# Regrouping the columns of an attention projection into panels of 512, 328, 512, 512 and 256, and loading the first tokens in two halves

## The chip, the cores and the metric

The kernel is written for Trainium2 and runs on one core. The metric is the device time of one execution, in microseconds (us). All times below come from timed runs of this kernel or from one execution that was taken with the hardware profiler.

## What is computed

The program is a decoder trunk of two layers over 512 tokens of width 1024, in float32. The change lies in the first layer's token mixer, a sparse attention:

```python
proj = x @ w_in                                   # 512 x 1024 times 1024 x 2120
q, k, v, iq, ik, iw = jnp.split(proj, A_SPLITS, axis=-1)   # 1024, 256, 256, 512, 64, 8 columns
q, k, iq, ik = partial_rotary(...)                # first 16 of the 64 numbers of each head
# for each block of 128 queries:
s = einsum('bqhd,bsd->bqhs', iq_b, ik) * IDX_DIM ** -0.5
score = einsum('bqh,bqhs->bqs', iw_b, relu(s))    # 8 index heads
_, sel = lax.top_k(where(causal, score, -inf), 128)
p = softmax(q_b @ k_sel)                          # 16 heads, 4 key heads
out = (p @ v_sel) @ w_o
x = layer_norm(alpha * x + out)
```

The 128 best keys of a query are all its causal keys for the first block of 128 queries. So token tile 0 needs no index queries and no index weights; it needs its index key, because later blocks look at it.

## The kernel before

**Tiles.** The 512 tokens are four token tiles of 128. `XT` holds x transposed, in a high and a low float32r part. A weight panel is up to 512 columns of a weight matrix over all 1024 rows. It comes as four units of 256 rows: `fetch` (L116) loads a unit into one of four `raw` buffers with one DMA on the queue of SyncE for each range of columns, and `split` (L125) makes the high part on ScalarE (L130) and the low part on VectorE (L131), into one of six `w` buffers. `natural` (L198) multiplies one token tile with a panel: 8 slices of 128 rows times three products (L186 to L188), so 24 matmuls whose length is the panel's width, into one of three PSUM tiles `ps`. `to_xt` (L223) turns a token tile into `XT` with 8 transposes, two ScalarE copies (L233) and two VectorE subtractions (L234). `next_panel` loads one panel ahead.

**Panels of the projection.** Five panels: 264 columns (three index query heads, the index key, the index weights), 320 columns (five index query heads), 512 (keys and values), 512 (query heads 0 to 7), 512 (query heads 8 to 15). Token tiles go in the order 1, 2, 3, 0 through the first panel (L632). Tile 0 takes only 64 of its columns there (L638), and the second panel leaves tile 0 out (L648). The panel list stands at L1074.

**After a product.** `rotated` (L546) copies and rotates the heads: one ScalarE copy (L554), three VectorE operations (L557 to L559). `stack_q` and `stack_k` split the result in two parts (L566 and L567; L584 to L586) and put transposes off by `depth` products (`later`, L190), which go to `iqT`, `ikT`, `kT` or `qT` through ScalarE (L575, L596).

**Selection and attention.** `index_scores(b)` (L616) makes the scores of block b, 8 heads with two matmuls, a ScalarE Relu and a VectorE accumulation each. It needs `iqT` of tile b and `ikT` of tiles 0 to b, so the first call stands behind the panels that hold the index queries and the index keys. `top_k` (L663) then takes 16 rounds of a maximum and a replacement on VectorE for each of the blocks 1 to 3 (L668, L669), closed by L671. `blocks` (L778) is a generator of 16 items, one for each block and key head: logits (L691 to L699), transposes of the weights (L706), the product with the values, and, at the end of a block, `to_xt` of its output. Items 8 to 11 are block 2 and items 12 to 15 block 3. Block 2 needs the selection of block 2, block 3 that of block 3. The code asks for all selections before item 8.

**Order.** SyncE's DMAs go in the order in which the program issues them. For the compute engines the framework takes the program and lays out each engine's order ahead of the run: earlier code comes first where it is ready by its own estimate, and later code moves forward where it isn't. The first product of the third panel, for example, stands on TensorE ahead of the first index scores, which the code names before it. Around the attention's end the code is:

```python
wu = self.next_panel()
for _ in range(A_KV):
    item()                      # items 8 to 11
self.load_residual(x)
for t in range(NT - 1):
    item()                      # items 12 to 14
    self.out_first(wu, t)       # output projection, first half, tile t
for _ in bl:
    pass
self.out_first(wu, NT - 1)
```

Of the kernel before, what the change touches and what calls it, by code (L numbers as in the profile page):

```python
# [23 lines left out]
P = 128  # L24
# [70 lines left out]
class Trunk:  # L95
# [29 lines left out]
    def split(self, src):  # L125
# [4 lines left out]
        self.nc.scalar.copy(hi, src)  # L130
        self.nc.vector.tensor_sub(lo, src, hi.bitcast(F32))  # L131
        return hi, lo

    def _load(self, i):
# [4 lines left out]
        for ci, (w, r0, nk, cols) in enumerate(panel):  # L139
            for u in range(nk // 2):  # L140
                hi, lo = self.split(self.fetch(w, r0 + 2 * u * P, cols))
                for j in range(2):
                    units[(ci, 2 * u + j)] = (hi[:, j, :], lo[:, j, :])
# [21 lines left out]
    def prefetch(self, n):  # L165
        while len(self.loaded) < min(len(self.panels), n):
            self.loaded.append(self._load(len(self.loaded)))
# [378 lines left out]
    def rotated(self, src, t, h):  # L546
# [3 lines left out]
        dst = self.rt.tile([P, self.rt_h, 64], F32, name="nat")[:, :h, :]  # L550
# [4 lines left out]
        a = self.rt.tile([P, self.rt_h, 2, 8], F32, name="rot_c")  # L555
        b = self.rt.tile([P, self.rt_h, 2, 8], F32, name="rot_s")
# [5 lines left out]
    def stack_q(self, nat, h, dst):  # L562

        nc = self.nc
        hl = self.rt.tile([P, self.rt_h, P], F32R, name="hl")
# [13 lines left out]
    def stack_k(self, nat, h, dst):  # L579

        nc = self.nc
        hl = self.rt.tile([P, h, 2, 2, 64], F32R, name="dup")
# [17 lines left out]
    def attention(self, x, xs):  # L600

        nc, tc = self.nc, self.tc
        with tc.tile_pool(name="att", bufs=1) as ap:
# [5 lines left out]
            with tc.tile_pool(name="idx", bufs=1) as ip, tc.tile_pool(name="ir", bufs=2) as it, \  # L609
                    tc.tile_pool(name="idt", bufs=3) as self.rt:  # L610
# [3 lines left out]
                self.rt_h, self.depth = 5, 2  # L614
# [17 lines left out]
                for i, t in enumerate(ORDER):  # L632
                    def turn_next(i=i):
                        if i + 1 < NT:
                            self.to_xt(xs[ORDER[i + 1]], ORDER[i + 1])
                    ik = ikT[:, None, :, t * P:(t + 1) * P]
                    if t == 0:
                        ps = self.natural(u, t, 192, 64)  # L638
                        self.stack_k(self.rotated(ps[:, 0:64], t, 1), 1, ik)
                    else:  # L640
                        ps = self.natural(u, t, 0, 264, turn_next)
                        nat = self.rotated(ps[:, 0:256], t, 4)
                        self.stack_q(nat[:, 0:3, :], 3, iqT[:, t - 1, 5:8, :])
                        self.stack_k(nat[:, 3:4, :], 1, ik)
                        nc.vector.tensor_scalar(iw[:, t, :], ps[:, 256:264], IDX_H ** -0.5, A_D ** -0.5,
# [524 lines left out]
```

## Time and profile before

| what | value |
|---|---|
| median of 3 runs | 1160.45 us (1160.43 to 1160.72) |
| profiled execution, own time | 1162.37 us |
| span of its profile | 1160.6 us |
| TensorE matmul busy | 1144.4 us, 99% |
| TensorE weight loads busy | 963.0 us, 83% |
| VectorE busy | 890.5 us, 77% |
| ScalarE busy | 556.9 us, 48% |
| granted TensorE clock, mean | 0.996 |

A share is that of the whole span, and matmuls overlap in the pipeline, so that a busy TensorE can still hide short waits. Where TensorE really runs without a break is seen from the distance between the starts of successive matmuls. PEclk is the granted share of TensorE's full clock of 2.4 GHz; 0.50 is 1.2 GHz.

### The profile page before, as it was taken

Reading aid. Unit: us, or ns where it says so; the run is one execution under the profiler, and the core shown is the slowest. Engines: PE = TensorE matmul, PEld = TensorE weight load, DVE = VectorE, ACT = ScalarE, POOL = GpSimd, SP = SyncE. Lnnn points to the kernel's source line nnn. Section 1 sums busy time; section 2 is a strip of 40 time slices with the busy share of each in tenths; the row PEclk is TensorE's granted clock in tenths of the full one; section 3 lists DMA queues with packets and bytes.
Section 4 is the critical chain, followed back from the end, with each engine's and each line's share of the span. In section 5 each row is a group of like instructions: output and inputs, shape, how many; then the busy total and the mean of one; then the engine's idle time right before and its main releaser. Section 6 shows DMA issues by size and latency. Waiting matters only on the chain. (4 is left out here: it accounts for less than half of the span.)

```text
span 1160.6 us, 15685 instructions
## 1 busy us (share of the span) xinstructions
PE 1144.4 (99%) x5847; PEld 963.0 (83%) x5847; DVE 890.5 (77%) x1587; ACT 556.9 (48%) x953; POOL 212.3 (18%) x144
## 2 busy tenths in 40 slices
PE   8999999999999999999999999999999999999997
PEld 7877888888888888888888998888988888888875
DVE  6799997687886786687864577766697866886787
ACT  6665786544444353344355444343453534444342
POOL 0000000002213203212302254110032032213221
PEclk9999999999999999999999999999999999999998
DMA  7322130521431441242241231233223422431421
GB/s 245 100 73 73 37 110 1 160 87 37 145 106 42 143 140 62 90 145 86 74 133 50 64 112 35 70 109 110 74 60 122 145 70 76 145 107 46 138 73 73
DMA packets 58196, 109.35 MB, mean 94 GB/s; under 512 B 5204, under 2 KB 10712, under 8 KB 58120
## 3 DMA queue, kind: packets, MB, share of 16 engines
q1 hardware_dynamic: 56968, 104.16, 28.1%
q0 software_dynamic: 1152, 4.19, 1.3%
q8 instruction: 46, 0.75, 0.3%
q14 instruction: 30, 0.25, 0.1%
HBM read 106.24 MB, written 2.10 MB: 93 GB/s over the span
## 5 line engine op out<-in xcount | busy, mean ns | idle before, releaser
L131 DVE TENSOR_TENSOR w_lo<-raw,w_hi 128x1024 fp32r<-128x1024 f32 (+4 forms) x220 | 289.3, 1333 | 27.5 <-ACT w_hi L130 25.1
L130 ACT CAST w_hi<-raw 128x1024 fp32r<-128x1024 f32 (+4 forms) x220 | 223.4, 1024 | 121.4 <-PE ps L188 43.8
L186 PE MATMUL ps<-XT,w_hi 128*128 128x512 f32 (+1 forms) x640 | 236.1, 369 | 0.0
L187 PE MATMUL ps<-XT,w_hi 128*128 128x512 f32 (+1 forms) x640 | 235.7, 368 | 0.0
L188 PE MATMUL ps<-XT,w_lo 128*128 128x512 f32 (+1 forms) x640 | 235.6, 368 | 0.0
L186 PE MATMUL ps<-w_hi,XT 128*128 128x512 f32 (+5 forms) x440 | 164.5, 374 | 0.8 <-ACT w_hi L130 0.8
L187 PE MATMUL ps<-w_lo,XT 128*128 128x512 f32 (+5 forms) x440 | 161.8, 368 | 1.1 <-DVE w_lo L131 1.1
L188 PE MATMUL ps<-w_hi,XT 128*128 128x512 f32 (+5 forms) x440 | 161.6, 368 | 0.0
L186 PEld LDWEIGHTS ps<-XT,w_hi 128*128 128x128 f32 x640 | 120.7, 189 | 20.2 <-issue 0.2
L187 PEld LDWEIGHTS ps<-XT,w_hi 128*128 128x128 f32 x640 | 120.7, 189 | 20.2 <-issue 0.4
L188 PEld LDWEIGHTS ps<-XT,w_lo 128*128 128x128 f32 x640 | 120.7, 189 | 20.1 <-issue 0.2
L152 POOL TENSOR_TENSOR raw<-raw 128x1024 f32<-128x1024 f32 x14 | 34.2, 2440 | 385.4 <-DVE w_lo L131 385.4
L186 PE MATMUL ps<-w_hi,form 128*128 128x512 f32 x260 | 102.3, 393 | 0.7 <-DVE big L408 0.7
L187 PE MATMUL ps<-w_lo,form 128*128 128x512 f32 x260 | 101.5, 390 | 0.0
L188 PE MATMUL ps<-w_hi,form 128*128 128x512 f32 x260 | 101.4, 390 | 0.0
L187 PEld LDWEIGHTS ps<-w_lo,XT 128*128 128x128 f32 x440 | 83.5, 190 | 11.9 <-DVE w_lo L131 1.7
L186 PEld LDWEIGHTS ps<-w_hi,XT 128*128 128x128 f32 x440 | 83.5, 190 | 11.5 <-ACT w_hi L130 1.0
L188 PEld LDWEIGHTS ps<-w_hi,XT 128*128 128x128 f32 x440 | 83.5, 190 | 10.8
L131 DVE TENSOR_TENSOR w_lo<-t,w_hi 128x1024 fp32r<-128x1024 f32 x14 | 30.4, 2168 | 72.7 <-ACT w_hi L130 72.7
L360 DVE TENSOR_TENSOR h<-h 128x512 f32<-128x512 f32 (+1 forms) x72 | 43.7, 624 | 44.1 <-ACT h L359 44.1
L359 ACT ACTIVATE h<-ps 128x512 f32<-128x512 f32 (+1 forms) x72 | 38.7, 546 | 61.7 <-PE ps L188 54.7
L130 ACT CAST w_hi<-t 128x1024 fp32r<-128x1024 f32 x14 | 14.7, 1051 | 105.2 <-POOL t L154 105.2
(238 smaller groups left out, 1986.1 us busy)
## 6 DMA issues: line engine op xcount, KB each, us to landing
raw<-in_mlp_w_up_dram SPq DMA_DIRECT2D x64, 512.0 KB, 4.5
raw<-in_mlp_w_down_dram SPq DMA_DIRECT2D x64, 512.0 KB, 4.6
raw<-in_b_w_in_dram SPq DMA_DIRECT2D x16, 512.0 KB, 4.6
raw<-in_a_w_in_dram SPq DMA_DIRECT2D x12, 512.0 KB, 4.3
big<-in_x_dram SPq DMA_DIRECT2D x8, 512.0 KB, 4.1
raw<-in_a_w_o_dram SPq DMA_DIRECT2D x8, 512.0 KB, 4.0
raw<-in_b_w_o_dram SPq DMA_DIRECT2D x8, 512.0 KB, 5.0
raw<-in_b_w_in_dram SPq DMA_DIRECT2D x8, 346.0 KB, 4.3
```

Source lines behind the costliest of these rows:

```text
L130: self.nc.scalar.copy(hi, src)
L131: self.nc.vector.tensor_sub(lo, src, hi.bitcast(F32))
L152: sub(t1, b12, b11)
L186: mmul(out, lhs[0], rhs[0], start=first, stop=False, skip_group_check=more)
L187: mmul(out, lhs[0], rhs[1], start=False, stop=False, skip_group_check=more)
L188: mmul(out, lhs[1], rhs[0], start=False, stop=last, skip_group_check=more)
L359: nc.scalar.activation(h, ps[:, :step], AF.Relu)
L360: nc.vector.tensor_mul(h, h, h)
```

## The change

The five panels become: 512 columns (all eight index query heads); 328 (keys, index key, index weights; two ranges of columns, 256 and 72); 512 (values, query heads 0 to 3); 512 (query heads 4 to 11); 256 (query heads 12 to 15). Token tiles 1, 2, 3 go through the first panel; all four tiles go through the other four. The index scores of block 1 move behind the second panel's four products, and those of blocks 2 and 3 stay inside the third panel. Of x's first token tile (tile 1) the two halves of 512 columns come with two DMAs. The DMA of the second token tile (tile 2) moves ahead of the last two units of the first panel. The first panel's units are split in two steps of one 128-row slice each. The buffers of the index stage's pool go from three to two, the `dup` tiles keep three, and tiles that held up to five heads now hold eight. `depth` is 1 in the first panel and 2 in the second.

```diff
-    def split(self, src):
+    def split(self, src, step=2):
...
-        self.nc.scalar.copy(hi, src)
-        self.nc.vector.tensor_sub(lo, src, hi.bitcast(F32))
+        for j in range(0, 2, step):
+            b = slice(j, j + step)
+            self.nc.scalar.copy(hi[:, b], src[:, b])
+            self.nc.vector.tensor_sub(lo[:, b], src[:, b], hi[:, b].bitcast(F32))
         return hi, lo
 
-    def _load(self, i):
+    def _load(self, i, amid=None):
...
         for ci, (w, r0, nk, cols) in enumerate(panel):
+            if ci and amid:
+                amid()
             for u in range(nk // 2):
-                hi, lo = self.split(self.fetch(w, r0 + 2 * u * P, cols))
+                hi, lo = self.split(self.fetch(w, r0 + 2 * u * P, cols), 1 if i == 0 else 2)
...
-        hl = self.rt.tile([P, h, 2, 2, 64], F32R, name="dup")
+        hl = self.rt.tile([P, h, 2, 2, 64], F32R, name=f"dup{h}", bufs=3)
...
-                    tc.tile_pool(name="idt", bufs=3) as self.rt:
+                    tc.tile_pool(name="idt", bufs=2) as self.rt:
...
-                for i, t in enumerate(ORDER):
+                for i, t in enumerate(ORDER[:-1]):
                     def turn_next(i=i):
-                        if i + 1 < NT:
-                            self.to_xt(xs[ORDER[i + 1]], ORDER[i + 1])
-                    ik = ikT[:, None, :, t * P:(t + 1) * P]
-                    if t == 0:
-                        ps = self.natural(u, t, 192, 64)
-                        self.stack_k(self.rotated(ps[:, 0:64], t, 1), 1, ik)
-                    else:
-                        ps = self.natural(u, t, 0, 264, turn_next)
-                        nat = self.rotated(ps[:, 0:256], t, 4)
-                        self.stack_q(nat[:, 0:3, :], 3, iqT[:, t - 1, 5:8, :])
-                        self.stack_k(nat[:, 3:4, :], 1, ik)
-                        nc.vector.tensor_scalar(iw[:, t, :], ps[:, 256:264], IDX_H ** -0.5, A_D ** -0.5,
+                        self.to_xt(xs[ORDER[i + 1]], ORDER[i + 1])
+                    ps = self.natural(u, t, 0, 512, turn_next)
+                    self.stack_q(self.rotated(ps, t, IDX_H), IDX_H, iqT[:, t - 1])
+                u = self.next_panel()
+                self.depth = 2
+                for t in range(NT):
+                    own = slice(t * P, (t + 1) * P)
+                    ps = self.natural(u, t, 0, 328)
+                    nat = self.rotated(ps[:, 0:320], t, A_KV + 1)
+                    self.stack_k(nat[:, A_KV:, :], 1, ikT[:, None, :, own])
+                    self.stack_k(nat[:, :A_KV, :], A_KV, kT[:, :, :, own])
+                    if t > 0:
+                        nc.vector.tensor_scalar(iw[:, t, :], ps[:, 320:328], IDX_H ** -0.5, A_D ** -0.5,
                                                 op0=OP.mult, op1=OP.mult)
-                u = self.next_panel()
-                for t in range(1, NT):
-                    ps = self.natural(u, t, 0, 320)
-                    self.stack_q(self.rotated(ps[:, 0:320], t, 5), 5, iqT[:, t - 1, 0:5, :])
-                    if t == 3:
-                        index_scores(1)
+                index_scores(1)
                 u = self.next_panel()
                 for t in range(NT):
                     ps = self.natural(u, t, 0, 512)
...
-                    nc.scalar.copy(vn[:, t, :, 0:64], ps[:, 256:512].rearrange("p (h d) -> p h d", d=64))
-                    self.stack_k(self.rotated(ps[:, 0:256], t, A_KV), A_KV, kT[:, :, :, t * P:(t + 1) * P])
+                    nc.scalar.copy(vn[:, t, :, 0:64], ps[:, 0:256].rearrange("p (h d) -> p h d", d=64))
+                    self.stack_q(self.rotated(ps[:, 256:512], t, 4), 4, qT[t][:, 0:4, :])
...
-                    self.stack_q(self.rotated(ps, t, 8), 8, qT[t][:, 0:8, :])
+                    self.stack_q(self.rotated(ps, t, 8), 8, qT[t][:, 4:12, :])
...
-                    ps = self.natural(u, t, 0, 512)
-                    self.stack_q(self.rotated(ps, t, 8), 8, qT[t][:, 8:16, :])
+                    ps = self.natural(u, t, 0, 256)
+                    self.stack_q(self.rotated(ps[:, :256], t, 4), 4, qT[t][:, 12:16, :])
...
-        T.panels = ([panel(wa, (1856, 264)), panel(wa, (C_IQ, 320)), panel(wa, (C_K, 512)), panel(wa, (0, 512)),
-                     panel(wa, (512, 512)), panel(wao, (0, 512)), panel(wao, (512, 512))] + mlp_panels(0)
+        T.panels = ([panel(wa, (C_IQ, 512)), panel(wa, (C_K, 256), (C_IK, 72)), panel(wa, (C_V, 256), (0, 256)),
+                     panel(wa, (256, 512)), panel(wa, (768, 256)), panel(wao, (0, 512)), panel(wao, (512, 512))] + mlp_panels(0)
...
-            nc.sync.dma_start(xs[first], x[first * P:(first + 1) * P, :])
-            T.prefetch(1)
+            for c in (0, 512):
+                nc.sync.dma_start(xs[first][:, c:c + 512], x[first * P:(first + 1) * P, c:c + 512])
+
+            def second():
+                t = ORDER[1]
+                nc.sync.dma_start(xs[t], x[t * P:(t + 1) * P, :])
+
+            T.prefetch(1, second)
...
-        for t in ORDER[1:]:
+        for t in ORDER[2:]:
             nc.sync.dma_start(xs[t], x[t * P:(t + 1) * P, :])
```

## Rows read from the trace of the kernel before

**Rows 1.** Busy time by stretch, PE, PEld, DVE, ACT, POOL; then clock, DMA share, GB/s.
```profile
5.37:13.17 7.80, 5.95 (x41) 4.98 (x41) 5.69 (x15) 4.75 (x11) 0.00 (x0) 1.00 1.02 374
13.17:37.59 24.42, 24.42 (x185) 24.32 (x183) 15.79 (x43) 16.17 (x39) 0.00 (x0) 0.93 0.51 170
37.59:104.00 66.41, 65.67 (x333) 52.67 (x333) 64.70 (x174) 40.39 (x80) 0.00 (x0) 1.00 0.26 85
104.00:149.60 45.60, 44.60 (x301) 38.32 (x299) 42.74 (x146) 33.26 (x68) 0.00 (x0) 1.00 0.18 56
...
168.90:215.20 46.30, 46.30 (x263) 38.25 (x261) 32.58 (x86) 31.54 (x76) 1.22 (x2) 1.00 0.14 45
```
**Rows 2.** Timeline: transposes, panel three's start, selection's end, first and last out_first.
```profile
37.22 0.54 PE L574 MATMUL tps<-ident_r,hl 128*128 128x128 f32 x5
37.59 0.46 PE L186 MATMUL ps<-w_hi,XT 128*128 128x512 f32 x1
...
149.61 0.42 DVE L671 TENSOR_SCALAR sc<-sc 128x512 f32<-128x512 f32 x1
...
177.50 0.40 PE L186 MATMUL ps<-w_hi,XT 128*128 128x512 f32 x1
...
215.18 0.50 PE L186 MATMUL ps<-w_hi,XT 128*128 128x512 f32 x1
```
**Rows 3.** Timeline, TensorE: first and last of runs of matmuls of one width.
```profile
21.61 0.27 PE L186 MATMUL ps<-w_hi,XT 128*128 128x64 f32 x1
...
23.84 0.28 PE L188 MATMUL ps<-w_hi,XT 128*128 128x64 f32 x1
...
25.00 0.47 PE L186 MATMUL ps<-w_hi,XT 128*128 128x320 f32 x1
...
27.93 0.45 PE L188 MATMUL ps<-w_hi,XT 128*128 128x320 f32 x1
...
30.13 0.31 PE L187 MATMUL ps<-w_lo,XT 128*128 128x320 f32 x1
...
33.35 0.31 PE L188 MATMUL ps<-w_hi,XT 128*128 128x320 f32 x1
...
129.24 0.39 PE L187 MATMUL ps<-w_lo,XT 128*128 128x512 f32 x1
...
134.25 0.39 PE L188 MATMUL ps<-w_hi,XT 128*128 128x512 f32 x1
```
**Rows 4.** First product's first and last matmul.
```profile
7.24 0.39 PE L186 MATMUL ps<-w_hi,XT 128*128 128x264 f32 x1 [0.77 <-ACT w_hi L130]
...
13.05 0.28 PE L188 MATMUL ps<-w_hi,XT 128*128 128x264 f32 x1
```
**Rows 5.** SyncE's issues of the first panel's fourth unit and x's last tile.
```profile
3.55 0.47 SPq L121 DMA_DIRECT2D raw<-in_a_w_in_dram  x1
...
5.30 0.59 SPq L1108 DMA_DIRECT2D big<-in_x_dram  x1
```
**Rows 6.** These two DMAs: size, median us from issue to landing.
```profile
raw<-in_a_w_in_dram SPq DMA_DIRECT2D x1, 264.0 KB, 6.0
...
big<-in_x_dram SPq DMA_DIRECT2D x1, 512.0 KB, 8.1
```
**Rows 7.** VectorE by line and shape, 0 to 200 us: busy, mean ns, idle before.
```profile
L131 DVE TENSOR_TENSOR w_lo<-raw,w_hi 128x1024 fp32r<-128x1024 f32 x18 | 21.6, 1219 | 1.4 <-ACT w_hi L130 1.3
L567 DVE TENSOR_TENSOR hl<-nat,hl 128x512 fp32r<-128x512 f32 x8 | 5.5, 683 | 0.0
L131 DVE TENSOR_TENSOR w_lo<-raw,w_hi 128x528 fp32r<-128x528 f32 x4 | 2.7, 701 | 0.8 <-ACT w_hi L130 0.8
L557 DVE TENSOR_TENSOR rot_c<-ps,cos 128x128 f32<-128x128 f32 x8 | 2.2, 279 | 0.6 <-ACT nat L554 0.5
L585 DVE TENSOR_TENSOR dup<-nat,dup 128x256 fp32r<-128x256 f32 x4 | 1.7, 414 | 0.0
L557 DVE TENSOR_TENSOR rot_c<-ps,cos 128x64 f32<-128x64 f32 x7 | 1.5, 218 | 0.2 <-ACT nat L554 0.2
```

More of the change, by code (lines that the diff above doesn't have):

```diff
@@ L163, in _load_forms, with prefetch @@
         return f
-    def prefetch(self, n):
+    def prefetch(self, n, amid=None):
         while len(self.loaded) < min(len(self.panels), n):
-            self.loaded.append(self._load(len(self.loaded)))
+            self.loaded.append(self._load(len(self.loaded), amid))
     def next_panel(self, ahead=1):
@@ L549, in rotated @@
         src = src.rearrange("p (h d) -> p h d", d=64)
-        dst = self.rt.tile([P, self.rt_h, 64], F32, name="nat")[:, :h, :]
+        dst = self.rt.tile([P, 8, 64], F32, name="nat")[:, :h, :]
         c = self.cos[:, t, None, None, :].to_broadcast([P, h, 2, 8])
@@ L554, in rotated @@
         nc.scalar.copy(dst[:, :, 16:64], src[:, :, 16:64])
-        a = self.rt.tile([P, self.rt_h, 2, 8], F32, name="rot_c")
-        b = self.rt.tile([P, self.rt_h, 2, 8], F32, name="rot_s")
+        a = self.rt.tile([P, 8, 2, 8], F32, name="rot_c")
+        b = self.rt.tile([P, 8, 2, 8], F32, name="rot_s")
         nc.vector.tensor_tensor(a[:, :h], x2, c, op=OP.mult)
@@ L564, in stack_q @@
         nc = self.nc
-        hl = self.rt.tile([P, self.rt_h, P], F32R, name="hl")
+        hl = self.rt.tile([P, 8, P], F32R, name="hl")
         nc.scalar.copy(hl[:, :h, 0:64], nat)
@@ L613, in attention @@
                 iw = ip.tile([P, NT, IDX_H], F32, name="iw")
-                self.rt_h, self.depth = 5, 2
                 def index_scores(b):
@@ L804, in attention @@
                     tc.tile_pool(name="pT", bufs=8) as ptp, tc.tile_pool(name="on", bufs=1) as op_:
-                self.rt_h = 8
                 tk, bl = top_k(), blocks()
```

## Prediction

> **What bounds the kernel now.** I read the busy time by stretch first [rows 1], because a share over the whole span says nothing about a change in the first 150 us. Look at three stretches. From 5.37 to 13.17 us TensorE is busy for 5.95 of 7.80 us while the DMA engines are busy throughout at 374 GB/s: the start is fed by DMA. From 13.17 to 37.59 us TensorE is busy all the time, at a mean clock of 0.93. From 37.59 to 149.60 us two engines are full at once: TensorE with 110.3 of 112.0 us and VectorE with 64.70 + 42.74 = 107.4 us, which leaves VectorE 4.6 us idle. After 168.90 VectorE has slack (32.6 of 46.3 us) and TensorE none.
>
> Then I read the marks in the timeline [rows 2]. The third panel starts at 37.59, and there the first index scores can start. VectorE closes the last selection at 149.61. The first output product starts at 177.50, the last at 215.18. So the question is what happens to the pair TensorE and VectorE between 37.59 and 149.61, and who is ahead at its end.
>
> **The products.** Pitches come from the first and last start of unbroken runs [rows 3]. 64 columns: 21 matmuls, (23.84 - 21.61) / 20 = 0.1115 us. 320 columns: 23 matmuls, (33.35 - 30.13) / 22 = 0.1464 us. 512 columns: 23 matmuls, (134.25 - 129.24) / 22 = 0.2277 us. Between the last two a column is worth 0.000423 us, which gives 0.1227 us for 264, 0.1498 for 328 and 0.1193 for 256. Before, in matmuls: 72 x 0.1227 + 24 x 0.1115 + 72 x 0.1464 + 288 x 0.2277 = 8.83 + 2.68 + 10.54 + 65.58 = 87.6 us. After, with the same 456 matmuls: 264 x 0.2277 + 96 x 0.1498 + 96 x 0.1193 = 60.11 + 14.38 + 11.45 = 85.9 us. That is -1.7 us. The 256 columns lie between the 64-column pitch (96 x 0.1115 = 10.7) and the one of 264 (11.8), so the term lies between -2.4 and -1.4.
>
> The row says that 64 columns cost nearly what 256 cost [rows 3]. The Trainium skill, page "TensorE: Matmul & The Clock Gate", section "Back-to-back issue gap", gives an isolated matmul its columns at 2.4 GHz plus 2.5 ns, so an estimate of 29 ns for 64 columns. By that the regrouping would bring nothing: the columns grow by 8 for one tile, 24 x 8 / 2.4 GHz = +0.1 us in place of -1.7. Its section on LDWEIGHTS gives 128 columns of weights 107 ns, and this the 0.1115 us agrees with. The measured pitch decides.
>
> **The clock.** Right after the narrow product of tile 0 the 320-column matmuls run at (27.93 - 25.00) / 11 = 0.266 us, twice the later pitch [rows 3], which is the level of 1.2 GHz; the mean of 0.93 shows this drop [rows 1]. Twelve matmuls at 0.120 us too much cost 1.4 us. No narrow product is left, so I take -1.4; the other bound is 0, if the clock falls elsewhere.
>
> **The start.** SyncE's queue is now: constants, two halves of x's first tile, two units, x's second tile, two units, x's other two tiles, constants. The additional DMA costs one issue, about 0.47 us [rows 5], for all that is queued behind it. The landings I take from the bytes ahead, since the data rate is the limit. Before, the fourth unit lands at 3.55 + 6.0 = 9.55 us with 68 + 512 + 4 x 264 = 1636 KB moved, and x's last tile at 5.30 + 8.1 = 13.4 us with 3172 KB [rows 5, 6]. After, the second unit needs 1604 KB, so about 9.5 us, and the fourth 3140 KB, so about 13.4 us. Its two slices then go through halves of the split: VectorE takes about 0.70 us for 528 elements [rows 7], so the last low part is there at about 13.4 + 0.6 + 2 x 0.7 = 15.4 us, and two more matmuls end the first product at 15.9 us. Before, its last matmul starts at 13.05 and the next product at about 13.2 [rows 4]. So it ends 2.7 us later, but 24 x (0.2277 - 0.1227) = 2.5 us of later work is in it. Net +0.2 us. Tile 2's first twelve matmuls need only the two early units and may fill the waits, which gains perhaps 0.6 us; if landings are later, it is up to +1. I take 0.
>
> TensorE's own sum is -1.7 - 1.4 + 0 = -3.1 us.
>
> **What moves on VectorE.** From the first product's end to the third panel TensorE needs 24.42 us before [rows 1], of which 48 x 0.1227 + 2.68 + 10.54 + 1.44 = 20.6 us are these products and the lost clock, and 3.9 us transposes. After: 2 x 24 x 0.2277 + 14.38 = 25.3 us, the same 3.9 us, and 17 more transposes (5 for index queries, 12 for keys) at (37.59 - 37.22) / 5 = 0.074 us [rows 2], 1.3 us. So the third panel starts at 15.9 + 25.3 + 3.9 + 1.3 = 46.4 us, 8.8 us later, and index scores and selections with it. On TensorE this is made good inside the attention, which has 10 us of products less. VectorE gets back less. Out of its full stretch go the keys' rotation and split, 4 x (3 x 0.218 + 0.414) = 4.3 us, and the shorter split of the last panel, 4 x (1.219 - 0.701) = 2.1 us [rows 7]. The query heads, before 8 x (3 x 0.279 + 0.683) = 12.2 us, become four calls of eight heads and eight of four: 6.1 + 8 x (3 x 0.218 + 0.414) = 14.6 us (the split of four heads has no row; the nearest is L585's 0.414). Net -4.3 - 2.1 + 2.4 = -3.9 us. So the selection's end moves by +8.8 - 3.9 = +4.9 us, less what VectorE's 4.6 us of idle time give back. Part of those are the short gaps between instructions, so I take half, and the end comes at +2.6 us (bounds +0.3 and +4.9). TensorE is then 3.1 + 2.6 = 5.7 us ahead of VectorE, and what it does with them decides the result.
>
> **The rest at nothing.** Two pool buffers for three: with `depth` 1 a tile is free when the next product ends, hidden behind a 5.5 us product; without cover, some tenths. Four more DMAs for the 328-column panel stand on SyncE's queue ahead of the third panel's, which is not needed before 46 us. ScalarE gets the keys' copies in a stretch where it has 8 us idle [rows 1]; if that is used up, up to 1 us more.
>
> **The rivals.** (A) VectorE ends the selections 2.6 us late and TensorE fills part of its lead with the first output product, 24 x 0.2277 = 5.5 us, which before stands only at 177.50 [rows 2]. For it: the framework moves later code forward, and after the selections TensorE is the only full engine. Against a full recovery: the product needs block 0's output, which comes late in this stretch. I take two thirds of it, 3.6 us: 2.6 - 3.6 = -1.0 us.
>
> (B) VectorE's lateness isn't felt, because the selections have slack towards block 3 or the whole product fills the lead. For it: block 3 needs the last selection later than 149.61. Then TensorE's sum counts: -3.1 us, 1157.3 us.
>
> (C) The other side: VectorE becomes the bound. Place: between the third panel's start and L671. Price: +2.6 us, up to +4.9, so 1163.1 to 1165.4 us. It decides if no output product starts ahead of the selections' end and blocks 2 and 3 wait for VectorE. For it: 107.4 of 112.0 us [rows 1]. The Trainium skill, page "Perfetto Trace Analysis", section "Identifying the Most-Contended Engine", says the same as a rule: judge VectorE by occupancy, TensorE by its weight loads, and work on the fuller one. The trace has VectorE at 96% and the weight loads at 81% in this stretch [rows 1], so by that rule shorter products bring nothing here.
>
> (D) The change doesn't do what it says: the clock falls anyway, in the start with its waits. Against: it stayed at 1.00 in the waits of 5.37 to 13.17 [rows 1]. Price +1.4 on A, so +0.4 us.
>
> **How the numbers follow.** The profiled execution has a span of 1160.6 us and takes 1162.37 us in all; A makes that 1161.4 us. The median of the runs is 1.9 us below it, 1160.45, and on that scale A is 1159.4 us. Chances: A 0.40, B 0.34, C 0.19, D 0.07. A measurement here can tell 0.2%, 2.3 us, from no change. A lies within it but for 0.04 on the fast side and 0.03 on the slow side; of B 0.32 is faster; of C 0.17 is slower; the rest and D are within. So faster 0.36, same 0.44, slower 0.20. A's own range is 1158.2 to 1161.4. The whole range goes from B with the lowest 256-column term and the filled start (-3.1 - 0.7 - 0.6 = -4.4, 1156.0) to the middle of C, 1163.6 us.
>
> **What the profile will show.** No stretch at half clock near 25 us; 328-column matmuls at 0.150 us and 256-column ones at 0.119; the first product's end near 15.9 us; the third panel's start near 46.4; L671's end near 152; an output product in pieces ahead of 177. What would make me wrong: landings that aren't ruled by the bytes ahead, index scores that start well before 46 us, or a selection that runs late without any wait on TensorE.

## The result, and the profile after

The changed kernel takes 1169.95 us (median of 4 runs, 1168.36 to 1170.67), the kernel before 1160.59 us beside it (4 runs, 1160.43 to 1162.27). The ratio is 1.0075, 95% interval 1.0058 to 1.0093: slower by about 9 us, and outside the predicted range, which ended at 1163.6. The profiled execution takes 1170.01 us, with a span of 1168.2 us against 1160.6. That is 7.6 us and not 9: the profiled execution of the kernel before was one of its slower ones, which experiment 1 explains.

The same marks as in [rows 2], from the timeline of the changed kernel, with three more: the first product's first matmul, the transposes of the third token tile (tile 3; behind 36 matmuls), and VectorE's first instruction on index scores.

```profile
9.78 0.79 PE L190 MATMUL ps<-w_hi,XT 128*128 128x512 f32 x1 [3.29 <-ACT w_hi L132]
...
21.78 1.04 PE L235 MATMUL tps<-cft,big 128*128 128x128 f32 x8
...
50.17 0.46 PE L190 MATMUL ps<-w_hi,XT 128*128 128x512 f32 x1
...
53.30 0.35 DVE L628 TENSOR_SCALAR sc<-r,iw 128x256 f32<-128x256 f32 x1
...
158.89 0.42 DVE L670 TENSOR_SCALAR sc<-sc 128x512 f32<-128x512 f32 x1
...
185.14 0.39 PE L190 MATMUL ps<-w_hi,XT 128*128 128x512 f32 x1
...
222.82 0.50 PE L190 MATMUL ps<-w_hi,XT 128*128 128x512 f32 x1
```

And the first instruction on index scores in the kernel before:

```profile
41.26 0.35 DVE L625 TENSOR_SCALAR sc<-r,iw 128x256 f32<-128x256 f32 x1
```

Read the shift at each mark. Panel three starts at 50.17, 12.6 us later. The first index score comes 12.0 us later, the end of the last selection 9.3 us later, the first output product 7.6 us later, the last one 7.6 us later, and so does the span's end. Nothing is won or lost behind that. So the start of panel three is the place to look at first, then what is given back between 53 and 159 us, and then what happens behind the selections.

Busy time by stretch in the changed kernel (columns as in [rows 1]):

```profile
5.00:10.00 5.00, 1.71 (x12) 1.20 (x10) 3.10 (x13) 2.20 (x6) 0.00 (x0) 0.86 0.96 350
10.00:15.40 5.40, 5.40 (x13) 3.79 (x14) 3.68 (x7) 2.66 (x6) 0.00 (x0) 0.50 1.04 398
15.40:37.84 22.44, 22.30 (x133) 19.25 (x132) 15.09 (x28) 14.36 (x26) 0.00 (x0) 1.00 0.61 173
...
150.00:160.00 10.00, 7.88 (x54) 6.15 (x54) 10.00 (x27) 5.57 (x13) 0.00 (x0) 1.00 0.25 100
160.00:170.00 10.00, 7.71 (x38) 6.50 (x39) 8.58 (x24) 6.17 (x16) 0.00 (x0) 0.83 0.35 105
...
53.30:158.90 105.60, 101.94 (x642) 86.65 (x642) 102.20 (x325) 69.74 (x147) 0.00 (x0) 1.00 0.20 64
158.90:222.80 63.90, 60.84 (x342) 50.47 (x341) 48.65 (x128) 44.08 (x108) 1.22 (x2) 0.97 0.15 50
...
8.56:15.37 6.81, 5.59 (x13) 3.98 (x14) 3.92 (x7) 3.55 (x7) 0.00 (x0) 0.50 1.03 396
...
162.16:165.58 3.42, 3.42 (x13) 3.00 (x13) 2.57 (x9) 2.54 (x7) 0.00 (x0) 0.50 0.48 148
```

In the start TensorE waits 3.29 us for the first weights and the clock is at 0.50 (1.2 GHz) from 8.56 to 15.37. No half clock is left where the narrow product was: 15.40 to 37.84 has 1.00, where [rows 1] had 0.93. From 150 to 170 us TensorE is idle for 4.4 of 20 us, where it had 0.5 us idle in all the 65.6 us behind the selections before, and VectorE has not a gap in the first ten of them. The timelines of VectorE and TensorE in the changed kernel show what it waits for there:

```profile
157.17 0.67 DVE L668 MATCH_REPLACE8 sc<-m,sc 128x512 f32<-128x512 f32 x1
157.76 1.21 DVE L133 TENSOR_TENSOR w_lo<-raw,w_hi 128x1024 fp32r<-128x1024 f32 x1
158.89 0.42 DVE L670 TENSOR_SCALAR sc<-sc 128x512 f32<-128x512 f32 x1
159.23 1.22 DVE L133 TENSOR_TENSOR w_lo<-raw,w_hi 128x1024 fp32r<-128x1024 f32 x1
160.36 1.22 DVE L744 TENSOR_TENSOR big<-vn,big 128x1024 fp32r<-128x1024 f32 x1
...
157.32 1.97 PE L723 MATMUL po<-vn,pT 128*128 128x65 f32 x16 [0.63 <-DVE on L726]
161.72 0.47 PE L756 MATMUL ps<-pT,big 128*128 128x512 f32 x1 [2.43 <-DVE big L744]
```

VectorE's queue has the last round, a weight split, the selection's closing step, another weight split and the split of the values (L744), one behind the other, and TensorE waits 2.43 us for the last of these. Soon behind this wait the clock is at 0.50, from 162.16 to 165.58 us. No piece of the first output product stands here; it starts at 185.14.

### The profile page after: what moved, and what is told of

Its sections match the earlier page's. It is cut to its first block, busy times and chain, and to the rows that moved or that the text cites. A ratio compares the mean times of both kernels' runs of the same rounds, so it can differ in the third digit from the quotient of the medians.

```text
span 1168.2 us, 15709 instructions
## 1 busy us (share of the span) xinstructions
PE 1146.2 (98%) x5847; PEld 964.2 (83%) x5847; DVE 891.0 (76%) x1592; ACT 558.9 (48%) x955; POOL 212.3 (18%) x144
## 3 DMA queue, kind: packets, MB, share of 16 engines
q1 hardware_dynamic: 59288, 104.16, 27.8%
## 5 line engine op out<-in xcount | busy, mean ns | idle before, releaser
L190 PE MATMUL ps<-w_hi,XT 128*128 128x512 f32 (+4 forms) x440 | 164.1, 373 | 3.3 <-ACT w_hi L132 3.3
L191 PE MATMUL ps<-w_lo,XT 128*128 128x512 f32 (+4 forms) x440 | 161.4, 367 | 0.0
L192 PE MATMUL ps<-w_hi,XT 128*128 128x512 f32 (+4 forms) x440 | 161.0, 366 | 0.0
L190 PEld LDWEIGHTS ps<-XT,w_hi 128*128 128x128 f32 x640 | 120.7, 189 | 20.3 <-issue 0.2
L191 PEld LDWEIGHTS ps<-XT,w_hi 128*128 128x128 f32 x640 | 120.7, 189 | 20.2 <-issue 0.4
L192 PEld LDWEIGHTS ps<-XT,w_lo 128*128 128x128 f32 x640 | 120.7, 189 | 20.1 <-issue 0.2
```

The source lines that it names most:

```text
L190: mmul(out, lhs[0], rhs[0], start=first, stop=False, skip_group_check=more)
L191: mmul(out, lhs[0], rhs[1], start=False, stop=False, skip_group_check=more)
L192: mmul(out, lhs[1], rhs[0], start=False, stop=last, skip_group_check=more)
```

## Experiments

Theory 1: VectorE is full from the first index score to the last selection, so this stretch has a fixed length; what starts it late ends it late, and TensorE waits for it. Part of the lateness is the start (a wait, then half clock), the rest the first two panels. The rivals: TensorE's own order and waits around 150 to 170 us cost the time, whatever comes ahead; the edits of the start cost it; a filler was there and was not taken. Each ratio is taken against runs of the kernel before on the same chip; the medians of that kernel differ by up to 2 us from experiment to experiment, for a reason that the first one shows. Where a kernel is said to be so much faster than the changed kernel, the medians are compared.

**1. The narrow product alone** (kernel before).

```diff
-                        ps = self.natural(u, t, 192, 64)
-                        self.stack_k(self.rotated(ps[:, 0:64], t, 1), 1, ik)
+                        ps = self.natural(u, t, 0, 264)
+                        self.stack_k(self.rotated(ps[:, 192:256], t, 1), 1, ik)
```

> The kernel before, with one edit: token tile 0 takes all 264 columns of the first panel in place of 64. This tests the clock step alone. If the half clock near 25 us in the kernel before comes from the narrow product, the 320-column matmuls behind it run at 0.146 us instead of 0.266 from the start (-1.4 us), and the 24 matmuls cost 24 x (0.1227 - 0.1115) = +0.3 us, so the third panel's first product starts about 1.1 us earlier, near 36.5 us, and the time falls by about 1 us to 1159.5, if the selections' end follows the third panel's start (theory 1: VectorE is the bound from there to the selections' end). If the clock falls for another reason, +0.3 us or nothing.

1161.05 us (10 runs, 1160.31 to 1161.13), ratio 0.9994 (0.9985 to 1.0004). In this kernel, busy time from the narrow product's place to panel three, and then from the timeline the second and the last matmul of its first 320-column product:

```profile
20.95:35.41 14.46, 14.46 (x111) 14.43 (x110) 8.57 (x20) 10.24 (x23) 0.00 (x0) 1.00 0.51 170
```

```profile
23.98 0.32 PE L187 MATMUL ps<-w_lo,XT 128*128 128x320 f32 x1
...
27.21 0.31 PE L188 MATMUL ps<-w_hi,XT 128*128 128x320 f32 x1
```

The clock is at 1.00, the pitch (27.21 - 23.98) / 22 = 0.147 us from the start, and the profiled execution takes 1160.35 us, 2.0 less than that of before. Panel three starts 2.2 us earlier, at 35.41; 0.9 of this stands already ahead of the narrow product, and 1.3 are found behind it, where 1.1 was expected. But the median hardly moves. In its 70 timed runs the kernel before took 1162.06 us or more 26 times and 1161.15 or less 44 times, nothing between; where the clock was noted, it was 0.997 in all of the upper group and 0.998 or 0.999 in 38 of 41 of the lower. The three kernels with tile 0 at 264 columns (here and in experiment 9) never came above 1161.72 in 32 runs. All three profiles of a kernel with the narrow product show the half clock there (before, its relieved form in experiment 5, and experiment 6). So the half clock behind it seems to come in about four executions of ten; the profiled one of before was such a one, and by its time the median one isn't. The executions that were only timed leave no trace that could show it.

**2. The smaller panel first** (changed kernel). The two loops over the token tiles change places with their `depth`, and all four tiles go through the first one; in the panel list:

```diff
-        T.panels = ([panel(wa, (C_IQ, 512)), panel(wa, (C_K, 256), (C_IK, 72)), panel(wa, (C_V, 256), (0, 256)),
+        T.panels = ([panel(wa, (C_K, 256), (C_IK, 72)), panel(wa, (C_IQ, 512)), panel(wa, (C_V, 256), (0, 256)),
```

> The changed kernel, with the panel of 328 columns first (for tiles 1, 2, 3, 0) and the panel of the 512 index query columns second (tiles 1, 2, 3). The first units are then 328 x 256 numbers and not 512 x 256, the same columns are computed, and the same work is left for later. Theory 1 (the start's wait for large first units costs 3.8 us, and VectorE passes each microsecond of a later third panel on to the end): the first product starts near 8 us and not 9.8, little or no half clock in it, the third panel's first product comes 3 to 4 us earlier than 50.2, and the time falls by 3 to 4 us, to about 1166. Rival (the loss lies in TensorE's own waits and half clock between 156 and 170 us, whatever comes ahead): at most -1 us.

1168.05 us (4 runs, 1166.22 to 1168.29), ratio 1.0054 (1.0039 to 1.0069), about 2 us less than the changed kernel, where 3 to 4 were expected. The first product starts at 8.59, the clock stays at 1.00 in the start, the first index score comes at 50.38 and the selection's end at 156.18, 2.9 and 2.7 us earlier. The wait behind VectorE is there as before (2.43 us), and the half clock that comes with it lasts twice as long, 157.5 to 164.3. Theory 1 holds in its kind; 0.7 us of the gain are lost at that wait.

**3. TensorE kept busy in the start** (changed kernel).

```diff
             T.to_xt(xs[first], first)
+            T.warm_up(zeros, 12)
```

> The changed kernel, with 12 matmuls on zeros behind the transposes of x's first tile, in the 3.3 us in which TensorE waits for the first weights; nothing else changes. Theory 1: if the half clock of 8.57 to 15.40 us follows from that wait, the clock stays at 1.00, 12 to 13 matmuls of 512 columns cost 0.228 us instead of 0.427, 2.4 us come back at the third panel's start and at the end, if VectorE passes them on. If the first product is set by the landings of its weights and not by the clock, TensorE only waits longer and the gain is under 1 us. Rival (the loss lies between 156 and 170 us): no change.

1167.97 us (4 runs, 1167.51 to 1168.49), ratio 1.0057 (1.0042 to 1.0072). The timeline of this kernel:

```profile
7.18 2.75 PE L500 MATMUL ps<-zeros 128*128 128x512 bf16 x12
9.65 0.52 PE L190 MATMUL ps<-w_hi,XT 128*128 128x512 f32 x1
10.34 0.50 PE L191 MATMUL ps<-w_lo,XT 128*128 128x512 f32 x1 [0.17 <-DVE w_lo L133]
...
12.53 0.39 PE L191 MATMUL ps<-w_lo,XT 128*128 128x512 f32 x1
...
19.70 1.03 PE L235 MATMUL tps<-cft,big 128*128 128x128 f32 x8
...
48.10 0.46 PE L190 MATMUL ps<-w_hi,XT 128*128 128x512 f32 x1
...
156.81 0.42 DVE L670 TENSOR_SCALAR sc<-sc 128x512 f32<-128x512 f32 x1
```

No half clock in the start, and the matmuls have a pitch of 0.23 us. Panel three starts 2.07 us earlier, the selection ends 2.08 earlier, the span ends 1.9 earlier. The first product's start hardly moves, since its weights set it. So 2.1 of the start's loss is clock, and VectorE's stretch passes it on whole.

**4. The filler, asked for early** (changed kernel).

```diff
                 wu = self.next_panel()
+                early = self.natural(wu, 0, 0, 512)
                 for _ in range(A_KV):
                     item()
...
                     item()
-                    self.out_first(wu, t)
+                    if t == 0:
+                        self.accumulate(self.xn[0], self.sums[0], 0, early, ALPHA)
+                    else:
+                        self.out_first(wu, t)
```

> The changed kernel, with the product of the first output panel with token tile 0 asked for ahead of attention items 8 to 11, and its accumulation left at item 12. It is 24 x 0.2277 = 5.5 us of work that waits neither for the selections of blocks 2 and 3 nor for their values. Theory 1 in the form of my prediction's case A (TensorE is ahead of VectorE at the selections' end and has only to be given work): the product fills the waits between 150 and 170 us, the half clock of 162.2 to 165.6 goes away, and the time falls by 3 to 5 us. Rival: its weights or its tile are not ready that early, or it delays VectorE's own chain: between -1 and +1 us.

1164.91 us (6 runs, 1163.94 to 1166.34), ratio 1.0029 (1.0017 to 1.0041), about 5 us less; in the profiled executions 3.7, of which 0.9 is there already at the first index score (52.44). Its timeline:

```profile
142.67 0.40 PE L190 MATMUL ps<-w_hi,XT 128*128 128x512 f32 x1
...
151.25 0.40 PE L192 MATMUL ps<-w_hi,XT 128*128 128x512 f32 x1
...
159.59 0.42 DVE L670 TENSOR_SCALAR sc<-sc 128x512 f32<-128x512 f32 x1
...
162.43 0.47 PE L756 MATMUL ps<-pT,big 128*128 128x512 f32 x1 [1.72 <-DVE big L744]
```

The product stands in pieces among the attention from 142.67 on. TensorE does have the time for it, and used it only when the code asked for it there. The wait for L744 is shorter but stays, and the half clock behind it comes all the same (164.2 to 167.6).

**5. VectorE relieved** (the changed kernel, and the kernel before as the control). Eight of the sixteen rounds of block 3's selection are left out.

```diff
...
-                        nc.vector.max(out=m8, in_=sc[b])
-                        nc.vector.match_replace(out=sc[b], in_to_replace=m8, in_values=sc[b], imm_value=NEG_TAKEN)
+                        if b < 3 or not 4 <= i < 12:
+                            nc.vector.max(out=m8, in_=sc[b])
+                            nc.vector.match_replace(out=sc[b], in_to_replace=m8, in_values=sc[b], imm_value=NEG_TAKEN)
```

> The changed kernel with 8 of the 16 rounds of block 3's selection left out (so only half of its best keys are taken out before the closing step; the output isn't the reference's). This takes 8 x (0.684 + 0.674 + 0.086) = 11.6 us from VectorE in the stretch in which it is full, and nothing from TensorE. Theory 1 (VectorE is the bound from the third panel's start to the end of the selections): the last selection ends near 147 us and not 158.9, TensorE's waits between 150 and 170 us (5.2 + 2.7 us more than its usual pitch, half clock among it) go away, and the time falls by 6 to 7.5 us, to 1162.5 to 1164; what is left over before is the start. Rival (TensorE's waits there come from something else, such as the buffers or the second panel of the output projection): less than 2 us.

> The kernel before, with the same 8 rounds of block 3's selection left out (the output isn't the reference's). The control: before, TensorE is busy 9.6 to 9.9 of 10 us between 150 and 170 us. Theory 1 (before, VectorE is at the edge but does not yet set the end): the last selection ends near 138 us and the time falls by 0.5 to 1.5 us at most. If VectorE set the end before too, it falls by several us, as much as in the changed kernel.

Changed kernel: 1161.75 us (10 runs, 1160.30 to 1162.96), ratio 1.0008 (0.9999 to 1.0018), so 8.2 us less than with all rounds. Kernel before: 1161.67 us (10 runs, 1160.80 to 1163.55), ratio 1.0010 (1.0000 to 1.0019), so nothing gained. The first product, the first index score and the later stretches of the relieved changed kernel:

```profile
8.60 0.50 PE L190 MATMUL ps<-w_hi,XT 128*128 128x512 f32 x1 [2.58 <-ACT w_hi L132]
...
50.40 0.35 DVE L628 TENSOR_SCALAR sc<-r,iw 128x256 f32<-128x256 f32 x1
```

```profile
150.00:160.00 10.00, 9.69 (x69) 8.51 (x67) 8.23 (x26) 8.14 (x23) 0.00 (x0) 1.00 0.00 2
160.00:170.00 10.00, 9.79 (x62) 8.33 (x62) 9.01 (x27) 9.01 (x25) 0.00 (x0) 1.00 0.27 104
```

TensorE's idle time there falls from 4.4 to 0.5 us, and the half clock goes. The selections' own end came far earlier than expected (131.0 and 120.7, not 147 and 138), since the framework lays VectorE's order out anew and put other work behind them; so those ends are not to be compared. And not all of the 8.2 us is VectorE's: in this profiled execution the first product starts 1.2 us earlier than in the changed kernel's, the clock stays at 1.00 in the start, and the first index score comes 2.9 us earlier, all ahead of the place of the edit. Of the 9.4 us between the two spans (1168.2 and 1158.8) that leaves 6.5 for the relief; how much of the 8.2 between the medians is the start's was not measured. So the larger part of the loss in the changed kernel is VectorE's, before VectorE did not set the end, and with VectorE out of the way the two medians are 0.1 us apart.

**6. The lateness alone** (kernel before).

```diff
-                    if t == 3:
-                        index_scores(1)
...
-                    if t < 2:
-                        index_scores(t + 2)
+                    if t > 0:
+                        index_scores(t)
```

> The kernel before, with one thing changed: the index scores of blocks 1, 2 and 3 are asked for behind the second, third and fourth product of panel three and not ahead of them. The work of every engine is the same; only the scores and the selections behind them start about two products, 2 x 24 x 0.2277 = 10.9 us, later. This is the changed kernel's main effect by itself, without new panels and without the new start. Theory 1 (VectorE is full from the first index scores to the end of the selections, so what starts it late ends it late): it gets some 3 us of key rotations to do in the meantime, the last selection ends 5 to 8 us later than 149.6, and the time rises by 3 to 7 us. Rival (the panels' order and shape on TensorE cost the time, not the lateness of the scores): no change within 1 us.

1166.70 us (4 runs, 1165.98 to 1167.78), ratio 1.0049 (1.0034 to 1.0064). Its timeline, and then its busy time by stretch:

```profile
50.52 0.35 DVE L625 TENSOR_SCALAR sc<-r,iw 128x256 f32<-128x256 f32 x1 [0.34 <-ACT r L623]
...
158.97 0.42 DVE L669 TENSOR_SCALAR sc<-sc 128x512 f32<-128x512 f32 x1
...
159.91 0.64 PE L689 MATMUL qk<-kT,big 128*128 128x384 f32 x1 [2.01 <-DVE mx L691]
```

```profile
150.00:160.00 10.00, 6.95 (x52) 5.74 (x51) 9.99 (x27) 4.59 (x13) 0.00 (x0) 1.00 0.28 92
160.00:170.00 10.00, 9.39 (x49) 7.86 (x50) 8.57 (x26) 8.09 (x22) 0.00 (x0) 0.83 0.20 60
```

The old panels and the old start, but the index scores 9.3 us later: VectorE without a gap at 150 to 160, TensorE's wait, the half clock behind it, and 6 us of time. This is the picture of the changed kernel without any of its new shapes. It also shows a slack: the selection ends 9.4 us later and the end of the span comes 5.4 later.

**7. The start as it was, and a helper for VectorE** (both on the changed kernel). The first takes back x's halves, the second tile's early DMA and the split in two steps; the second puts the low parts of panels four to seven on GpSimd (of its edit the two lines that matter):

```diff
...
-            self.nc.vector.tensor_sub(lo[:, b], src[:, b], hi[:, b].bitcast(F32))
+            (eng or self.nc.vector).tensor_sub(lo[:, b], src[:, b], hi[:, b].bitcast(F32))
...
+                                    self.nc.gpsimd if 3 <= i <= 6 else None)
```

> The changed kernel with the start as it was: x's first tile in one DMA, the second tile's DMA behind the first panel's four units, and whole units split at once. The first panel still has 512 columns. If the three edits of the start cost time (an additional DMA and the half steps in front of the first product), the first product starts earlier than 9.78 us and the time falls by up to 3.8 us. If they give back something of what the larger units cost, the first product's second half comes later, the half clock lasts longer, and the time rises by 1 to 3 us. Theory 1 puts the loss on the size of the units, so it expects the second, or no change within 1 us; either way the shift of the third panel's start is found again at the end.

> The changed kernel, with the low parts of the weights of panels four to seven (the last 512 and the 256 query columns, and the output projection's two halves) on GpSimd and not on VectorE; the result is the same. It takes 12 x 1.215 + 4 x 0.678 = 17.3 us from VectorE between 50 and 160 us and gives GpSimd 12 instructions of the size of its subtractions elsewhere in the kernel (2.44 to 2.53 us) and four of half of it. Theory 1: about 15 us of it lie ahead of the selections' end, which moves to about 145 us, and the time falls by 5 to 7.5 us. Rival: GpSimd and VectorE slow each other down when both run, or the weights come too late; then the gain is under 2 us, or the time rises.

The old start: 1168.56 us (4 runs, 1167.77 to 1170.53), ratio 1.0069 (1.0054 to 1.0084). The intervals overlap with the changed kernel's. Panel three starts at 49.32, 0.9 us earlier, and the half clock is there too: the three edits did not cause the loss, and they win nothing that can be seen. The helper: 1177.34 us (4 runs, 1175.11 to 1179.86), ratio 1.0148 (1.0125 to 1.0171), 7 us worse; the rival held. What held VectorE and TensorE up there is in the last section.

**8 and 9. Combinations.** The edits of 2 and 4 together; those of 1 and 4 together on the kernel before; that of 1 with the three edits of the start.

> The changed kernel with two edits that were run apart: the 328-column panel first (1.9 us less) and the first output product asked for ahead of items 8 to 11 (5.0 us less). If they act on different losses (the one on the start, the other on TensorE's wait behind VectorE), they add up to -6 to -7 us, 1163 to 1164 us, still above before. If the filler takes the same wait that the earlier start shortens, they give no more than the better one, about 1165 us.

> The kernel before with both small edits that an experiment spoke for: tile 0 with all 264 columns (no half clock near 25 us), and the first output product asked for ahead of items 8 to 11. Theory 1: before, TensorE is busy 9.6 to 9.9 of 10 us between 150 and 170 us, so the filler has next to nothing to fill: between -0.5 and +0.5 us beside the 264 columns alone, about 1160 us. If it is over 1 us faster than that, TensorE waited for VectorE before, too.

> The kernel before with tile 0 at all 264 columns and with the changed kernel's three edits of the start (x's first tile in two DMAs, the second tile's DMA ahead of the last two units, the first panel's units split in halves), on units of 264 columns. It asks what these three edits are worth where the units are small. If they help as meant, the first product starts and ends some tenths earlier than with the 264 columns alone, and the time falls by 0.3 to 1 us, to about 1159.5. If the additional DMA and the half steps cost more than they bring (in the changed kernel, the start without them was at most 1.4 us faster), it is 0 to 1 us slower than the 264 columns alone. TensorE has no wait behind VectorE in this kernel, so whatever the start wins or loses should be found again at the end.

Smaller panel and filler: 1165.41 us (6 runs, 1161.80 to 1165.57), ratio 1.0033 (1.0021 to 1.0045). They don't add up in the median. One execution of the six, the profiled one, has no half clock and takes 1161.80; the other five lie between 1165.01 and 1165.57 at a mean clock of 0.995 to 0.996. On the kernel before, 264 columns and filler: 1160.17 us (11 runs, 1159.46 to 1160.57), ratio 0.9991 (0.9983 to 1.0000), the fastest kernel here, though at the edge of what can be told from no change. With the three edits of the start: 1160.88 us (11 runs, 1160.37 to 1161.72), ratio 1.0001 (0.9992 to 1.0010), nothing.

The length of VectorE's stretch over the kernels with all rounds, from the rows at its two ends:

| kernel | first index score | selection's end | length |
|---|---|---|---|
| before | 41.26 | 149.61 | 108.35 |
| 1, tile 0 at 264 columns | 39.08 | 147.43 | 108.35 |
| 6, scores asked for later | 50.52 | 158.97 | 108.45 |
| changed | 53.30 | 158.89 | 105.59 |
| 3, start kept busy | 51.21 | 156.81 | 105.60 |
| 2, smaller panel first | 50.38 | 156.18 | 105.80 |
| 7, old start | 52.65 | 158.20 | 105.55 |
| 4, filler | 52.44 | 159.59 | 107.15 |
| 7, helper | 51.98 | 158.99 | 107.01 |
| 8, smaller panel first and filler | 49.44 | 156.75 | 107.31 |
| 9, 264 columns and filler | 39.48 | 148.39 | 108.91 |
| 9, 264 columns and edits of the start | 39.18 | 147.53 | 108.35 |

A start 2.2 us earlier or 9.3 us later leaves it at 108.4; the new panels take 2.8 us out of it. That is theory 1 in a table, with three limits. The filler lengthens the stretch (+1.5 in the changed kernel, +0.6 in the kernel before), which the theory did not say. So does the helper (+1.4), which was to shorten it. And the idle time in the stretch can take work, though it doesn't shorten it: in experiment 6 VectorE is busy for 105.02 us of it and before for 103.78, at the same length.

## Why the prediction was wrong

The case that came is C, VectorE as the bound, with 0.19, and beyond its top: it was priced at +2.6 to +4.9 us and came to 9. (The range's top of 1163.6 is called the middle of C; the middle of 1163.1 and 1165.4 is 1164.2, which the result exceeds as well.) The likeliest, A, did not happen. Three steps failed: the start was put at 0 and was 3.8 us late in the profile, VectorE's idle time gave back 0.6 us and not 2.3, and TensorE did not fill its lead by itself (0 and not 3.6), so that it waited for VectorE. By the prediction's steps:

- **The products, -1.7: right.** The 328-column matmuls run at (36.70 - 33.41) / 22 = 0.150 us, those of 256 columns at (135.45 - 132.81) / 22 = 0.120, the first and last of a run in each. The sum is 86.0 us where 85.9 was said. It bought nothing: TensorE waited for VectorE, and with VectorE relieved (experiment 5) it doesn't show between the medians either.
- **The clock, -1.4: the mechanism right, its base wrong.** The half clock near 25 us goes with the narrow product, as experiment 1 shows. But the sum was made against the profiled execution and then put on the scale of the median by its 1.9 us, as if that distance were a constant. It was mostly this same half clock. By its time, the median had none of it to give back.
- **The start, 0: the first large miss, 3.8 us** (panel three at 50.17, not 46.4). The first product starts at 9.78; the larger first unit makes TensorE wait 3.29 us, with 6.8 us of half clock from within the wait on. 2.1 us of the miss are the clock (experiment 3). Of the other 1.7, 1.1 stand ahead of the transposes of tile 3, which by the sum come behind 36 matmuls, at 15.9 + 12 x 0.2277 = 18.6 us, and in experiment 3 come at 19.70. Most of that is tile 2's eight transposes: in the kernel before they stand among the first product's waits (at 11.33 us), and here for 0.79 us between matmuls that hardly wait. The last 0.6 are behind that mark: from there to panel three it takes 28.4 us in both kernels, and the sum has 36 x 0.2277 + 14.38 + 3.9 + 1.3 = 27.8, so transposes cost more than was said. The size of the miss is also that of one execution: with the same start, panel three came at 49.31, 48.80 and 47.28 in the profiles of experiments 4, 7 (helper) and 5, where the first weights came earlier and 3 us of half clock or none followed. Three of the four timed runs of the changed kernel have the profiled one's mean clock, 0.993. Rival D had said that the clock may fall in the start, at +1.4 on A with 0.07, and argued against it with a start whose waits were shorter [rows 1, 4].
- **The lateness of panel three, +8.8 by itself: right**, and it is the core of the loss. Experiment 6 makes 6 us of time out of 9.3 us of lateness alone.
- **"VectorE's idle time gives back half", -2.3: wrong, it gave 0.6.** From panel three's start to the selection's end VectorE is idle for 112.02 - 107.45 = 4.6 us before and 108.72 - 104.75 = 4.0 us in the changed kernel. Before, it was busy throughout from panel three's start to the first index score at 41.26; all of its idle time is gaps behind that, inside the stretch, and a later start hardly closes them.
- **VectorE's work, -3.9: too large, it was -2.7** (107.45 to 104.75 us). Part of what went out was made up by three more of block 2's logits (L692 in place of L693, 1.6 us), which now come ahead of the selection's end. With these, the selection's end is 2.6 + 3.8 + 1.7 + 1.2 = +9.3 us, as measured.
- **"TensorE fills its lead with the first output product", -3.6: wrong as a forecast, right in size.** The product stands at 185.14, not pulled ahead. The framework did not move it over items 8 to 12, which the code names first. Asked for early it gave 3.7 us in the profile, 0.9 of it from an earlier start, and 5.0 between the medians (experiment 4).
- **What a late selection costs behind its end.** It can slip some: by 9.3 us it costs 7.6, in experiment 6 by 9.4 it costs 5.4. From the selection's end to the last output product's start it is 65.6 us before, 63.9 in the changed kernel and 61.6 in experiment 6: TensorE has less left to do, and loses part of that in the waits and the half clock that follows. By itself, a slip of the size forecast (+2.6) might have cost nothing, as B said; that was not tried.

The rule of the Trainium skill that stood beside C (page "Perfetto Trace Analysis", section "Identifying the Most-Contended Engine"), to work on the fuller of two engines, agrees with the runs: where VectorE had 96%, shorter products on TensorE brought nothing, and 11.6 us off VectorE brought 6.5 in the profile. I had given C only 0.19, and had counted half of the 4.6 us of idle time as slack.

## What to carry to other kernels

Where two engines are full in one stretch, a change that saves work on one and starts the other later is judged by the later start: take the second engine's stretch as of fixed length first, and count its idle time as slack only if one row shows it in one piece at the place that moves. Before setting a gain against the median, look at whether the profiled execution has the loss that you mean to remove and the median one has it too. And count a product as filler only if the program asks for it at that place; here it was not moved there by itself.

## What the runs showed of the hardware

The clock fell at short waits, but not each time. In the start of the changed kernel it went to 0.50 at 8.56 us, 2 us into a wait of 3.29 us; in experiment 4 it fell behind a wait of 2.18 us at the same place, and in experiment 5 it stayed at 1.00 through one of 2.58 us, with the same program up to there. In the changed kernel and experiments 4 and 6 it fell 0.1 to 1.8 us after a wait of 1.7 to 2.4 us behind VectorE had ended, with TensorE busy again; in experiment 2 it fell within the wait. In experiment 8 the profiled execution kept 1.00 through a wait of 1.74 us at that place, and was 3.2 to 3.8 us faster than the other five. Their mean clock was lower (0.995 to 0.996 against 0.998), but where it fell in them no trace shows.

GpSimd's subtractions held VectorE up in experiment 7. The timelines of GpSimd and VectorE in that kernel:

```profile
141.87 10.55 POOL L133 TENSOR_TENSOR w_lo<-raw,w_hi 128x1024 fp32r<-128x1024 f32 x4 [23.16 <-ACT w_hi L132]
...
140.25 0.68 DVE L668 MAX8 m<-sc 128x8 f32<-128x512 f32 x1
...
143.08 2.28 DVE L572 TENSOR_TENSOR hl<-nat,hl 128x256 fp32r<-128x256 f32 x1 [0.22 <-ACT hl L571]
145.28 0.21 DVE L562 TENSOR_TENSOR rot_c<-ps,cos 128x64 f32<-128x64 f32 x1
...
145.89 1.77 DVE L564 TENSOR_TENSOR nat<-rot_c,rot_s 128x64 f32<-128x64 f32 x1
...
150.95 0.69 DVE L668 MAX8 m<-sc 128x8 f32<-128x512 f32 x1
```

While GpSimd subtracts, one L572 takes 2.28 us and one L564 1.77; in the changed kernel the same two take 0.42 and 0.21 (there L571 and L563). Both read two operands from SBUF. L562, with one operand in PSUM, and MAX8 at 150.95, with one operand, take what they take elsewhere. The Trainium skill, page "SBUF — State Buffer", section "Who interferes with whom", says that a VectorE instruction with two SBUF inputs contends with a GpSimd instruction that reads SBUF, that the ports which the two share are an exclusive lock, and that one with at most one SBUF input, outside the two-port modes, doesn't contend. These rows agree: the long ones take 1.6 to 1.9 us more than elsewhere, which is less than one whole subtraction of GpSimd (2.40 us by itself). TensorE waits for L572 in turn, by that kernel's list of waits from 50 to 230 us (total, times, longest):

```profile
PE tps L579 <- DVE hl L572: 6.0, 3, 2.8
```

The clock is at 0.83 and 0.82 in its stretches 140 to 150 and 150 to 160 us, too. How much of the 7 us comes from each was not separated.
